# A recurrence planned among dense projections: key norms with tokens on partitions, two PSUM banks told apart, longer pauses, and one projection moved

## The chip, the cores and the metric

The kernel runs on one core of a Trainium2 chip. The metric is the device time of one execution in microseconds; the median of three runs of the kernel before is 1794.55 us (1793.61 to 1795.46). A change of less than 0.2% can't be told from none here.

## The reference, cut to what matters

One layer takes 1040 tokens (16 learned ones ahead of 1024) of width 1024 through a norm and one wide projection, two branches beside each other, an output projection, and a gated feed-forward part. The first branch is stick-breaking attention with 8 heads of 64; the second is a recurrence with 8 heads of 64. The lines on the recurrence that the change touches are these:

```python
rw = token_shift(rw, mu_rw[layer])
r, kr, vr, w_lo, a_lo, g_lo = jnp.split(rw, rw_splits, axis=-1)
w_log = -jax.nn.softplus(-(w0[layer] + jnp.tanh(w_lo) @ w_up[layer])) - 0.5
decay = jnp.exp(-jnp.exp(w_log.astype(jnp.float32)))
a = jax.nn.sigmoid(a0[layer] + a_lo @ a_up[layer])
g = jax.nn.sigmoid(g_lo) @ g_up[layer]
kk = split_heads((kr * k_k[layer]).astype(jnp.float32), RW_HEADS)
kk = kk / jnp.maximum(jnp.linalg.norm(kk, axis=-1, keepdims=True), 1e-12)
...
y_rw = rwkv7_recurrence(r_h, split_heads(decay, RW_HEADS), k_h, v_h, kk, a_h)
y_rw = group_norm_heads(y_rw, ln_x_w[layer], ln_x_b[layer])
```

The norm of a key is one number for each token and head.

## The kernel before

The start normalises the tokens and transposes them into `xhi` and `xlo`, a high and a low part; every dense projection is three matmuls (hi by hi, lo by hi, hi by lo) for each of eight slices of the width, in pieces of 346 or 348 tokens, or 512 where the 16 first tokens aren't needed. `wload` fetches a weight tile, casts its high part on ScalarE and subtracts for the low part (`wlo`) on VectorE, or on GpSimd once `LOP[0]` is set.

First come, each drained before the next, the column of the decay and of `a` (`wa`, lines 283 to 285), the gate (`g_cols`: two projections, their sigmoids, the splits of the results, then the products `psg`), and key, receptance and value of the first pair of heads. `LOP[0]` is set between `wa` and `g_cols`.

The recurrence runs in chunks of 64 tokens, for four pairs of heads, each in two units of 9 and 8 chunks: eight units. Three chains of steps work on them: `chain1` (`stage1`: decay, key norms, the matrices within each chunk), `chain2` (`stage2a`: the inverse of each chunk's triangular matrix, in which a small 16 by 16 inversion `Tt` is done on VectorE in 30 short instructions) and `chain3` (`stage2b`: the pass over the chunks, one `psC` step each, then a group norm and the transposes `psyT`). Every step ends in a `yield` of two numbers: its cost on TensorE and a pause. A planner (lines 719 to 745) keeps a clock of its own: it takes the next step of a chain whose pause is over, in the order chain3, chain2, chain1, and else one slice of a dense projection (`psm`, three matmuls, 3 x (columns + 34) / 2400). In this way the remaining 28 columns of the attention and its gates, and the next pairs' keys, receptances and values, fill the pauses. The order so found is fixed for TensorE alone; the other engines' orders are left to a scheduler. When the chains end, what is left of the dense work is drained, and the attention begins (`psv`, `psz`, then on VectorE the scan L795 and the product L796, the transposes `psaT`, the products `pso`).

PSUM is dealt out by tags: `mm` has 3 banks (dense), A has 2, B, C and S one each. Chain1 uses A, chain2 uses A and B in turn, chain3 and the attention use C and S.

The norm of the keys in `stage1` works on the keys' own layout, channels on partitions: the squares `sq` (128 by 576 or 512) are multiplied by `blk1`, whose two blocks of ones add up 64 channels and repeat each sum on 64 partitions; the square root, the maximum with 1e-12 and the reciprocal then run on the full 128 by 576 or 512, and the product `kkn` follows behind a pause of 20:

Of the kernel before, what the change touches and what calls it, by code (L numbers as in the profile page):

```python
# [13 lines left out]
AF = mybir.ActivationFunctionType  # L14
ALU = mybir.AluOpType
# [79 lines left out]
def _build(nc, tc, I, out, dbg, es):  # L95
# [183 lines left out]
    def drain(g):  # L279
        for _ in g:  # L280
            pass

    wa = rp.tile([128, LP], F32, name="wa")
    drain(proj_shift(I["win"][0], 0, wa))
    A.activation(wa[0:64], wa[0:64], AF.Tanh)

# [13 lines left out]
    def tl(nm, shape, tag=None, **kw):  # L300
        return rp.tile(shape, F32, tag=tag or nm, name=nm, **kw)
# [6 lines left out]
    def stage1(p, u, rkv):  # L308
# [12 lines left out]
        for a, m in pcs:  # L321
            ps = bank("A", "psw")
            T.matmul(ps[:, :m * 64], waup[0:64, 128 * p:128 * p + 128], wa[0:64, t0 + a * 64:t0 + (a + m) * 64],
                     start=True, stop=True)
            A.activation(sg[:, a:a + m, 1:65], u3(ps[:, :m * 64]), AF.Sigmoid, bias=CV(W0, p))
            ps = bank("A", "psa")
            T.matmul(ps[:, :m * 64], waup[64:128, 128 * p:128 * p + 128],
                     wa[64:128, t0 + a * 64:t0 + (a + m) * 64], start=True, stop=True)
            A.activation(at[:, a * 64:(a + m) * 64], ps[:, :m * 64], AF.Sigmoid, bias=CV(A0, p))
            yield 0.75, 1.2  # L330
        cc = tl("cc", [128, n, 65])
# [9 lines left out]

        nv = tl("nv", [128, w], "sg")
        kkn = tl("kkn", [128, w])
        for a, m in pcs:
            ps = bank("A", "psn")
            T.matmul(ps[:, :m * 64], blk1, sq[:, a * 64:(a + m) * 64], start=True, stop=True)
            A.activation(nv[:, a * 64:(a + m) * 64], ps[:, :m * 64], AF.Sqrt)
        for a in range(0, w, w // 4):
            sl = slice(a, a + w // 4)
            V.tensor_scalar(nv[:, sl], nv[:, sl], 1e-12, None, op0=ALU.max)  # L350
            V.reciprocal(nv[:, sl], nv[:, sl])
        yield 0.6, 20.0
        V.scalar_tensor_tensor(kkn, krs, CV(KK, p), nv, op0=ALU.mult, op1=ALU.mult)
        m1 = sq
# [19 lines left out]
        for c in range(0, n, 4):  # L374
            m = min(4, n - c)
            pss = [bank("A", "pss") for h in range(2)]
            for c_ in range(c, c + m):
                o = (c_ - c) * 128
                for h in range(2):
                    q = HQ[h]  # L380
                    T.matmul(pss[h][:, o:o + 128], BK[q, c_].rearrange("p s x -> p (s x)"), AV[q, c_, h:3:2 - h],
                             start=True, stop=True)
            late = 2.4 if m > 1 else 1.2
            for h in range(2):
# [22 lines left out]
    def stage2a(p, u, s1):  # L407
# [9 lines left out]
        for a in range(0, n, 8):  # L417
            m = min(8, n - a)
            ps = bank("B", "psW")
            for c in range(a, a + m):  # L420
                o = (c - a) * 64
                for h in range(2):
                    T.matmul(ps[HQ[h], o:o + 64], UA[HQ[1 - h], c, h], X[HQ[1 - h], c, h], start=True, stop=True)
            A.copy(X[:, a:a + m, 2], u3(ps[:, :m * 64]))
            yield 0.09 * m + 0.2, 1.2

# [21 lines left out]

        yield 0.0, 19.0
        R32 = [(h, b, slice(64 * h + 32 * b, 64 * h + 32 * b + 32)) for b in range(2) for h in range(2)]  # L450
        Xq = t2("Xq", [128, 9, 32], "Tt")
        ps = bank("B", "psU")
        for c in range(n):
            for h, b, rows in R32:
                T.matmul(ps[rows, c * 32:c * 32 + 32], UA[rows, c, h, 32 * b:32 * b + 32], TN[rows, c],
                         start=True, stop=True)
        yield 1.9, 1.3
        V.tensor_tensor(Xq[:, :n], ps[:, :n * 32].rearrange("p (c x) -> p c x", x=32),
                        qmask.unsqueeze(1).to_broadcast([128, n, 32]), op=ALU.mult)
        ps = bank("A", "psU2")  # L460
        for c in range(n):
            for h, b, rows in R32:
                T.matmul(ps[rows, c * 32:c * 32 + 32], Xq[rows, c], TT[rows, c, 32 * b:32 * b + 32],
                         start=True, stop=True)
        yield 1.9, 2.4
        pv = ps[:, :n * 32].rearrange("p (c x) -> p c x", x=32)
# [14 lines left out]
        for h in range(2):  # L481
            (A.copy, V.tensor_copy)[h](Xs[QB[h], :n], ps[QB[h], :n * 32].rearrange("p (c x) -> p c x", x=32))
        yield 1.0, 1.3
        ps = bank("A", "psX2")
        for c in range(n):
            for h in range(2):
                T.matmul(ps[QA[h], c * 32:c * 32 + 32], Xs[QB[h], c], TT[QB[h], c, 32:64], start=True, stop=True)
        for h in range(2):
            (A.copy, V.tensor_copy)[h](TT[QA[h], :n, 32:64], ps[QA[h], :n * 32].rearrange("p (c x) -> p c x", x=32))
        yield 1.0, 1.3  # L490

        Pt = t2("Pt", [128, 9, 64])
        GM = t2("GM", [128, 9, 128], "UA", bufs=3)
        for c in range(0, n, 4):
# [9 lines left out]
            for h in range(2):  # L504
                A.copy(X[HQ[h], c:c + m, h], pv[HQ[h], :, 1])
            yield 0.2 * m, 1.6
            ps = bank("A", "psEF")
            for c_ in range(c, c + m):
                o = (c_ - c) * 128
                for h in range(2):  # L510
# [5 lines left out]
                            op=ALU.add)  # L516
            yield 0.15 * m, 0.0
        return GM

    def stage2b(p, u, s1, GM, St):  # L520
# [5 lines left out]
        for c in range(n):  # L526
# [11 lines left out]
            if g > 0:  # L538
                o = (g - 1) % 8
                A.copy(Yt[64 * (o % 2):64 * (o % 2) + 64, o // 2], cp_[0:64, 0:128])  # L540
            yield 0.45, 1.3

# [48 lines left out]
    def g_cols():  # L591
# [20 lines left out]
        split(u3_[0:32], u3_[64:96], ur)  # L612
        A.copy(u3_[32:64], ur)
        for p in range(4):
            if p % 2 == 0:
# [53 lines left out]
    def chain3():  # L669
        St = None  # L670
        for i_ in range(NU):
            yield (lambda: i_ in st2), 1.6
            if i_ % 2 == 0:
                St = None
            St = yield from stage2b(i_ // 2, i_ % 2, st1[i_], st2[i_], St)
            yd[i_] = True
# [389 lines left out]
    with ExitStack() as s4:  # L1066
        w5 = pool(s4, "w5")
        ft = lambda nm, bufs, dt=F32: w5.tile([128, 512], dt, tag=nm, name=nm, bufs=bufs)
# [99 lines left out]
```

## Time and profile before

| | us |
|---|---|
| median of three runs | 1794.55 |
| the profiled execution | 1788.92 |
| its span | 1787.2 |
| TensorE busy | 1706.4 (95%) |
| VectorE busy | 1171.1 (66%) |
| ScalarE busy | 770.3 (43%) |
| GpSimd busy | 387.0 (22%) |

The profile is of one execution; times in it run from the span's start. The first 33 us hold the first norm and its transposes; the chains run from about 115 to 718 us; dense work alone follows to about 770; the attention and the branch projections to 1020, the output projection and the second norm to 1130, the feed-forward part to the end. In the rows below, PE is TensorE, DVE VectorE, ACT ScalarE, POOL GpSimd; PEld is the loading of weights into TensorE. What stands behind an arrow is what an engine waited for.

### The profile page before, as it was taken

How to read it: one execution, taken by the hardware profiler on the slowest of the kernel's cores; microseconds unless marked ns; L12 is line 12 of the kernel's file. 1: busy time of each engine (PE TensorE's matmuls, PEld its weight loads, DVE VectorE, ACT ScalarE, POOL GpSimd, SP SyncE). 2: the span in 40 equal slices, each digit the busy share in tenths (PEclk: the TensorE clock that was granted, in tenths of full speed). 3: DMA queues.
4: the chain of work that ended last, by engine and by line, in shares of the span. 5: the costliest groups of instructions: out<-in, count | busy, mean ns of one | idle time of the engine just before them, and what ended most of it. 6: DMA issues, size and time to landing. Idle time of an engine off the chain costs nothing.

```text
span 1787.2 us, 28844 instructions
## 1 busy us (share of the span) xinstructions
PE 1706.4 (95%) x11120; PEld 1407.7 (79%) x11120; DVE 1171.1 (66%) x1969; ACT 770.3 (43%) x1542; POOL 387.0 (22%) x393
## 2 busy tenths in 40 slices
PE   7999999999999999998989999999999999999998
PEld 6787888888897788866666887788888888778886
DVE  6345654655655632078988844898887877579756
ACT  7344354444545533256655323532333332254445
POOL 2222112211111221300000001365454544210000
PEclk9999989999999999999999999999999999999999
DMA  5223213211211354225422535133333323297233
GB/s 173 71 77 97 70 49 95 57 54 40 80 41 50 94 127 127 89 74 129 119 72 63 180 129 189 50 116 100 107 118 100 106 89 100 93 323 250 89 107 129
DMA packets 98249, 188.79 MB, mean 106 GB/s; under 512 B 38592, under 2 KB 40912, under 8 KB 98112
## 3 DMA queue, kind: packets, MB, share of 16 engines
q1 hardware_dynamic: 83536, 139.63, 26.5%
q0 software_dynamic: 14576, 47.32, 7.0%
q8 instruction: 88, 1.44, 0.3%
q14 instruction: 49, 0.40, 0.1%
HBM read 133.49 MB, written 53.41 MB: 105 GB/s over the span
## 4 chain that ended last, share of the span: by engine, by line
PE 76%; DVE 12%; ACT 5%; issue 4%; DMA 3%; SPq 1%; POOL 0%; ACTq 0%; DVEq 0%; POOLq 0%
PE psf L959 8%; PE psf L958 8%; PE psm L254 8%; PE psf L957 8%; PE psm L255 7%; PE psm L256 7%; PE psfo L1120 4%; PE psfo L1121 4%; PE psfo L1119 4%; DVE ub L795 3%; DVE be L796 2%; PE psC L530 1%; PE pso L814 1%; PE psaT L804 1%; PE pswo L906 1%
## 5 line engine op out<-in xcount | busy, mean ns | idle before, releaser
L254 PE MATMUL psm<-xhi,whi 128*128 128x346 f32 (+3 forms) x872 | 326.8, 375 | 2.6 <-DVE stagel L147 1.8
L255 PE MATMUL psm<-xlo,whi 128*128 128x346 f32 (+3 forms) x872 | 308.7, 354 | 0.3 <-DVE xlo L147 0.3
L256 PE MATMUL psm<-xhi,wlo 128*128 128x346 f32 (+3 forms) x872 | 308.5, 354 | 0.0
L254 PEld LDWEIGHTS psm<-xhi,whi 128*128 128x128 f32 (+1 forms) x872 | 166.0, 190 | 30.4 <-issue 10.7
L256 PEld LDWEIGHTS psm<-xhi,wlo 128*128 128x128 f32 (+1 forms) x872 | 165.5, 190 | 15.5
L255 PEld LDWEIGHTS psm<-xlo,whi 128*128 128x128 f32 (+1 forms) x872 | 166.2, 191 | 13.8 <-DVE xlo L147 0.7
L156 POOL TENSOR_TENSOR wlo<-wraw,whi 128x1024 fp32r<-128x1024 f32 (+1 forms) x42 | 100.3, 2389 | 290.7 <-ACT whi L155 257.4
L1119 PE MATMUL psfo<-wh,ah 128*128 128x512 f32 x308 | 120.7, 392 | 2.5 <-ACT wh L146 2.5
L1120 PE MATMUL psfo<-wl,ah 128*128 128x512 f32 x308 | 121.0, 393 | 2.2 <-DVE wl L147 2.2
L1121 PE MATMUL psfo<-wh,al 128*128 128x512 f32 x308 | 120.8, 392 | 0.0
L146 ACT CAST sh<-S 128x512 fp32r<-128x512 f32 x88 | 54.5, 622 | 144.5 <-PE psf L958 135.8
L155 ACT CAST whi<-wraw 128x1024 fp32r<-128x1024 f32 (+2 forms) x71 | 67.0, 943 | 96.6 <-PE psm L255 36.0
L795 DVE TENSOR_TENSOR_SCAN ub<-ub 128x144 f32<-128x144 f32 (+7 forms) x64 | 87.7, 1381 | 4.2 <-ACT ub L792 4.2
L1047 DVE TENSOR_TENSOR g<-g,sg 128x512 f32<-128x512 f32 x44 | 78.4, 1781 | 15.5 <-ACT sg L1046 14.0
L146 ACT CAST ah<-ar 128x512 fp32r<-128x512 f32 x77 | 47.9, 622 | 92.5 <-PE psfo L1120 58.7
L147 DVE TENSOR_TENSOR al<-ar,ah 128x512 fp32r<-128x512 f32 x77 | 56.5, 734 | 42.4 <-ACT ah L146 42.3
L156 DVE TENSOR_TENSOR wlo<-wraw,whi 128x512 fp32r<-128x512 f32 (+1 forms) x29 | 28.4, 979 | 74.8 <-ACT whi L155 74.8
L147 DVE TENSOR_TENSOR sl<-S,sh 128x512 fp32r<-128x512 f32 x85 | 74.8, 881 | 0.0
L1119 PEld LDWEIGHTS psfo<-wh,ah 128*128 128x128 f32 x308 | 58.4, 190 | 15.1 <-ACT wh L146 2.9
L1120 PEld LDWEIGHTS psfo<-wl,ah 128*128 128x128 f32 x308 | 58.4, 190 | 14.6 <-DVE wl L147 2.5
L1121 PEld LDWEIGHTS psfo<-wh,al 128*128 128x128 f32 x308 | 58.4, 190 | 12.2
L536 DVE TENSOR_SCALAR Sbd<-psC,gam 64x64 f32<-64x64 f32 x64 | 18.5, 289 | 74.5 <-PE psC L533 73.8
(386 smaller groups left out, 4197.0 us busy)
## 6 DMA issues: line engine op xcount, KB each, us to landing
wr<-in_wffi SPq DMA_DIRECT2D x46, 512.0 KB, 3.6
wraw<-in_win SPq DMA_DIRECT2D x42, 512.0 KB, 3.9
ar<-d_a SPq DMA_DIRECT2D x77, 256.0 KB, 2.8
d_a<-sa POOLq DMA_DIRECT2D x44, 256.0 KB, 2.8
wf<-in_wffo SPq DMA_DIRECT2D x44, 256.0 KB, 5.3
d_a<-sg POOLq DMA_DIRECT2D x33, 256.0 KB, 2.4
d_g<-stage POOLq DMA_DIRECT2D x32, 256.0 KB, 3.1
gt<-d_g SPq DMA_DIRECT2D x32, 256.0 KB, 2.6
```

Source lines behind the costliest of these rows:

```text
L147: V.tensor_tensor(lo, src, hi.bitcast(F32), op=ALU.subtract)
L156: (G if LOP[0] else V).tensor_tensor(lo, raw, hi.bitcast(F32), op=ALU.subtract)
L254: T.matmul(ps[:M, :n], hv[:, k], xhi[:, k, t0:t0 + n], start=(k == 0), stop=False)
L255: T.matmul(ps[:M, :n], hv[:, k], xlo[:, k, t0:t0 + n], start=False, stop=False)
L256: T.matmul(ps[:M, :n], lv[:, k], xhi[:, k, t0:t0 + n], start=False, stop=(k == 7))
L795: V.tensor_tensor_scan(rv, rv, rv, 1.0, op0=ALU.mult, op1=ALU.bypass)
L957: T.matmul(ps, wa_[0][:, kc], xa_[0][:, k], start=(k == 0), stop=False)
L958: T.matmul(ps, wa_[0][:, kc], xa_[1][:, k], start=False, stop=False)
L959: T.matmul(ps, wa_[1][:, kc], xa_[0][:, k], start=False, stop=(k == 3))
L1119: T.matmul(ps, ah[:, tt], wh, start=(i == 0), stop=False)
L1120: T.matmul(ps, ah[:, tt], wl, start=False, stop=False)
L1121: T.matmul(ps, al[:, tt], wh, start=False, stop=(i == NP - 1))
```

## The change

It has five parts. The projection of `wa` and its Tanh move into `g_cols`, between the splits and the products `psg`. The key norms get tokens on partitions: a block of 96 (or 128) tokens of `sq` is the stationary operand and two columns of `blk1` the moving one, so one small matmul gives the block's norms for two heads; root, maximum and reciprocal run on 96 by 12 (or 128 by 8); ScalarE copies them out to 64 columns each (`bt`); and a new step of transposes (`psnt`, six or four a unit) brings them to the keys' layout, where `kkn` reads them from PSUM. `psU2`, `psX2` and `psEF` of chain2 move from bank tag A to B. The planner's pauses change, most of them upwards. The pool `w5` of the last stage is laid at the other side of the memory.

```diff
     wa = rp.tile([128, LP], F32, name="wa")
-    drain(proj_shift(I["win"][0], 0, wa))
-    A.activation(wa[0:64], wa[0:64], AF.Tanh)
...
-            yield 0.75, 1.2
+            yield 0.75, 2.0
...
-        nv = tl("nv", [128, w], "sg")
+        tb = 96 if n == 9 else 128
+        nb = w // tb
+        nv = tl("nv", [128, 6, 2])[:tb, :nb]
+        bt = tl("bt", [128, 9, 2, 64], "BK").rearrange("p c s x -> p (c s x)")[:tb, 0:nb * 128]
         kkn = tl("kkn", [128, w])
-        for a, m in pcs:
-            ps = bank("A", "psn")
-            T.matmul(ps[:, :m * 64], blk1, sq[:, a * 64:(a + m) * 64], start=True, stop=True)
-            A.activation(nv[:, a * 64:(a + m) * 64], ps[:, :m * 64], AF.Sqrt)
-        for a in range(0, w, w // 4):
-            sl = slice(a, a + w // 4)
-            V.tensor_scalar(nv[:, sl], nv[:, sl], 1e-12, None, op0=ALU.max)
-            V.reciprocal(nv[:, sl], nv[:, sl])
-        yield 0.6, 20.0
-        V.scalar_tensor_tensor(kkn, krs, CV(KK, p), nv, op0=ALU.mult, op1=ALU.mult)
+        ps = bank("A", "psn")
+        pv = ps[:tb, 0:2 * nb].rearrange("p (b h) -> p b h", h=2)
+        for b in range(nb):
+            T.matmul(pv[:, b], sq[:, b * tb:(b + 1) * tb], blk1[:, 0:128:64], start=True, stop=True)
+        A.activation(nv, pv, AF.Sqrt)
+        V.tensor_scalar(nv, nv, 1e-12, None, op0=ALU.max)
+        V.reciprocal(nv, nv)
+        A.copy(bt.rearrange("p (b h x) -> p b h x", h=2, x=64), nv.unsqueeze(3).to_broadcast([tb, nb, 2, 64]))
+        yield 0.2 * nb, 3.4
+        for a in range(0, nb, nb // 2):
+            ps = bank("A", "psnt")
+            for b in range(a, a + nb // 2):
+                T.transpose(ps[:, (b - a) * tb:(b - a + 1) * tb], bt[:, 128 * b:128 * b + 128], ident[:tb, :tb])
+            sl = slice(a * tb, (a + nb // 2) * tb)
+            V.scalar_tensor_tensor(kkn[:, sl], krs[:, sl], CV(KK, p), ps[:, :nb // 2 * tb], op0=ALU.mult, op1=ALU.mult)
+        yield 0.11 * nb, 14.0
...
-            late = 2.4 if m > 1 else 1.2
+            late = 3.0 if m > 1 else 2.0
...
-        yield 1.9, 1.3
+        yield 1.2, 2.0
...
-        ps = bank("A", "psU2")
+        ps = bank("B", "psU2")
...
-        yield 1.9, 2.4
+        yield 1.2, 3.0
...
-        yield 1.0, 1.3
-        ps = bank("A", "psX2")
+        yield 0.9, 2.0
+        ps = bank("B", "psX2")
...
-            yield 0.2 * m, 1.6
-            ps = bank("A", "psEF")
+            yield 0.25 * m, 2.2
+            ps = bank("B", "psEF")
...
-            yield 0.15 * m, 0.0
+            yield 0.25 * m, 1.9
...
-            yield 0.45, 1.3
+            yield 0.45, 1.4
...
+
+        drain(proj_shift(I["win"][0], 0, wa))
+        A.activation(wa[0:64], wa[0:64], AF.Tanh)
         for p in range(4):
...
-            yield (lambda: i_ in st2), 1.6
+            yield (lambda: i_ in st2), 0.5
...
-        w5 = pool(s4, "w5")
+        w5 = pool(s4, "w5", side="right")
```

Line numbers differ between the two kernels behind line 283. The first place is TensorE at the gate's products, before; `psm` with 32 rows is the second gate projection, L621 to L623 are the parts of `psg` that need the first one's split, and L624 is the part that needs the second one's:

```order
L256 MATMUL psm<-xhi,wlo 32x346
L621 MATMUL psg<-gpr,gat 128x512
...
L623 MATMUL psg<-gpr,gcc 128x512
L624 MATMUL psg<-gUA,gsq 128x512 x5
L621 MATMUL psg<-gpr,gat 128x512
```

After the change the same place reads so (L632 to L635 are the old L621 to L624):

```order
L255 MATMUL psm<-xlo,whi 32x346
L256 MATMUL psm<-xhi,wlo 32x346
L254 MATMUL psm<-xhi,whi 128x348
...
L256 MATMUL psm<-xhi,wlo 128x346
L632 MATMUL psg<-gpr,gat 128x512
L633 MATMUL psg<-gAV,gat 128x512
L634 MATMUL psg<-gpr,gcc 128x512
L635 MATMUL psg<-gUA,gsq 128x512
```

The 72 matmuls of `wa`, with 128 rows, now stand between the second gate projection and its first use; before, they stood ahead of both.

The second place is ScalarE at the norm of the first unit, before; `E` and `cc` are the two exponentials of the decay, `nv` the roots of the norms, `gam` the decay at the ends of chunks:

```order
L334 ACT_TABLE_LOAD
L334 ACTIVATE E<-cc 128x585
L347 ACT_TABLE_LOAD
L347 ACTIVATE nv<-psn 128x320
L336 ACT_TABLE_LOAD
L336 ACTIVATE cc<-cc 128x9x64
L340 COPY gam<-E 64x9 x2
L347 ACT_TABLE_LOAD
L347 ACTIVATE nv<-psn 128x256
L146 CAST stageh<-psm 128x512
```

After the change (the copy `bt` reads the reciprocals that VectorE makes of `nv`, and the transposes `psnt` read `bt`):

```order
L332 ACT_TABLE_LOAD
L332 ACTIVATE E<-cc 128x585
L350 ACT_TABLE_LOAD
L350 ACTIVATE nv<-psn 96x12
L334 ACT_TABLE_LOAD
L334 ACTIVATE cc<-cc 128x9x64
L338 COPY gam<-E 64x9 x2
L353 COPY bt<-nv 96x768
L146 CAST stageh<-psm 128x512
```

Four table loads became three, and the exponential `cc` and the copies `gam` stand between the small root and the copy that TensorE's new step needs.

The third place is TensorE at the end of the chains, before; `psC` is a step over one chunk, `psyT` the transposes behind the last group norm, `psv` the attention's first instruction:

```order
L530 MATMUL psC<-X,UB 128x64 x2
L533 MATMUL psC<-Sbd_352,GM 128x128
L254 MATMUL psm<-xhi,whi 128x512
...
L256 MATMUL psm<-xhi,wlo 128x512
L558 MATMUL psyT<-ident,Yt 128x128 x4
L254 MATMUL psm<-xhi,whi 128x512
...
L256 MATMUL psm<-xhi,wlo 128x512
L762 MATMUL psv<-ident,vt 16x128
```

After the change (`psz`, `psaT` and `pso` are of the attention):

```order
L256 MATMUL psm<-xhi,wlo 128x512
L538 MATMUL psC<-X,UB 128x64 x2
L541 MATMUL psC<-Sbd_351,GM 128x128
L538 MATMUL psC<-X,UB 128x64 x2
L773 MATMUL psv<-ident,vt 16x128
...
L541 MATMUL psC<-Sbd_352,GM 128x128
L815 MATMUL psaT<-ident,be 16x128
...
L815 MATMUL psaT<-ident,be 128x128 x3
L566 MATMUL psyT<-ident,Yt 128x128 x4
L799 MATMUL psz<-kh,qs 128x264
L800 MATMUL psz<-kl,qs 128x264
L825 MATMUL pso<-aT_7657,vn 64x128
```

Before, 222 dense matmuls follow the last `psyT`. After, the last dense matmul stands ahead of the first of the last unit's eight `psC` steps; the other seven and `psyT` are placed among the attention's first instructions, and the first `pso` behind `psyT`.

## Rows read from the trace of the kernel before

**Rows 1.** Stretches: length; busy PE, PEld, DVE, ACT, POOL (instructions); clock; DMA.

```profile
160.00:660.00 500.00, 475.33 (x4618) 411.72 (x4618) 290.73 (x737) 237.93 (x484) 91.31 (x95) 0.97 0.24 66
720.00:765.00 45.00, 45.00 (x196) 36.38 (x195) 1.19 (x2) 8.41 (x13) 11.41 (x11) 1.00 0.28 91
765.00:1020.00 255.00, 232.71 (x1745) 175.96 (x1744) 217.96 (x317) 146.33 (x407) 1.93 (x7) 1.00 0.38 108
770.00:810.00 40.00, 36.14 (x288) 26.17 (x287) 39.48 (x60) 30.75 (x92) 0.89 (x4) 1.00 0.31 92
```

**Rows 2.** Waits of TensorE: releaser, us in total, times, longest.

```profile
PE psg L624 <- DVE gUA L147: 3.6, 1, 3.6
...
PE psa L327 <- ACT TT L469: 2.5, 2, 1.3
PE psn L346 <- DVE TT L489: 2.4, 2, 2.0
```

**Rows 3.** Narrow stretches: length, busy TensorE (instructions), granted clock, DMA share, GB/s.

```profile
66.30:73.10 6.80, 5.93 (x14) 0.50 0.36 146
250.60:260.80 10.20, 9.80 (x88) 0.50 0.13 46
547.60:551.00 3.40, 3.40 (x21) 0.51 0.00 0
```

**Rows 4.** Timeline of TensorE at the gate's products: start, duration, row.

```profile
63.14 0.40 PE L623 MATMUL psg<-gpr,gcc 128*128 128x512 f32 x1
67.17 2.47 PE L624 MATMUL psg<-gUA,gsq 96*128 96x512 f32 x5 [3.63 <-DVE gUA L147]
```

**Rows 5.** Groups by line: weight splits on two engines, reciprocal of the norms.

```profile
L156 POOL TENSOR_TENSOR wlo<-wraw,whi 128x1024 fp32r<-128x1024 f32 (+1 forms) x42 | 100.3, 2389 | 290.7 <-ACT whi L155 257.4 <-PE psC L533 17.8 <-PE psU L455 12.2
L351 DVE RECIPROCAL nv<-nv 128x144 f32<-128x144 f32 (+1 forms) x32 | 29.7, 968 | 0.0
L156 DVE TENSOR_TENSOR wlo<-wraw,whi 128x512 fp32r<-128x512 f32 (+1 forms) x29 | 28.4, 979 | 74.8 <-ACT whi L155 74.8
```

**Rows 6.** Timeline of ScalarE at the second unit's norm.

```profile
167.00 0.64 ACT L334 ACTIVATE E<-cc 128x520 f32<-128x520 f32 x1
...
168.01 0.63 ACT L336 ACTIVATE cc<-cc 128x512 f32<-128x512 f32 x1
...
169.09 1.28 ACT L347 ACT_TABLE_LOAD   x1
170.38 0.66 ACT L347 ACTIVATE nv<-psn 128x256 f32<-128x256 f32 x2
```

**Rows 7.** Timeline of VectorE at the same place.

```profile
166.58 0.14 DVE L435 TENSOR_TENSOR Tm<-Z,Tt 72x15 f32<-72x15 f32 x1
...
168.98 0.68 DVE L368 TENSOR_TENSOR AV<-r,E 128x512 f32<-128x512 f32 x1
```

**Rows 8.** Timeline of TensorE: second unit's last psa and psn; four transposes.

```profile
164.44 0.38 PE L327 MATMUL psa<-wa,waup 64*128 64x256 f32 x1
...
166.62 1.02 PE L346 MATMUL psn<-sq,blk 128*128 128x256 f32 x4
...
192.60 0.60 PE L394 MATMUL pst<-ident,AV 128*128 128x128 f32 x4
```

**Rows 9.** Timeline of all engines: last unit's steps, its norm's two ends.

```profile
703.72 0.55 PE L530 MATMUL psC<-X,UB 128*128 128x64 f32 x4
...
704.11 0.44 PE L533 MATMUL psC<-Sbd,GM 128*128 128x128 f32 x2
...
704.59 0.29 DVE L536 TENSOR_SCALAR Sbd<-psC,gam 64x64 f32<-64x64 f32 x1 [1.76 <-PE psC L533]
...
704.91 0.31 ACT L537 ACTIVATE Sbd<-psC,gam 64x64 f32<-64x64 f32 x1 [1.46 <-DVE Sbd L536]
...
708.72 0.26 ACT L540 COPY Yt<-psC 64x128 f32<-64x128 f32 x1 [0.66 <-PE psC L533]
...
717.63 0.60 PE L558 MATMUL psyT<-ident,Yt 128*128 128x128 f32 x4
```

More of the change, by code (lines that the diff above doesn't have):

```diff
@@ L424, in stage2a @@
             A.copy(X[:, a:a + m, 2], u3(ps[:, :m * 64]))
-            yield 0.09 * m + 0.2, 1.2
+            yield 0.09 * m + 0.2, 1.8
         Z = t2("Z", [128, 288], "Z")[:npb, 0:256].rearrange("p (i t) -> p i t", t=16)
@@ L447, in stage2a @@
             SY.dma_start(TT[rows, :n, 16 * b:16 * b + 16], dt_[ib].rearrange("c j t -> j c t"))
-        yield 0.0, 19.0
+        yield 0.0, 20.0
         R32 = [(h, b, slice(64 * h + 32 * b, 64 * h + 32 * b + 32)) for b in range(2) for h in range(2)]
@@ L489, in stage2a @@
             (A.copy, V.tensor_copy)[h](TT[QA[h], :n, 32:64], ps[QA[h], :n * 32].rearrange("p (c x) -> p c x", x=32))
-        yield 1.0, 1.3
+        yield 0.9, 2.0
         Pt = t2("Pt", [128, 9, 64])
```

## The prediction

> **What bounds the kernel now.** I read the stretches of the span first [rows 1]. While the chains run, 160 to 660 us, TensorE is busy 475.33 of 500: it is the bound, with 24.7 us of holes. From 720 to 765 it does dense work alone, 45.00 of 45, while VectorE has 1.19 of work; 196 matmuls of 512 columns in 45 us are 0.23 us each. In the attention TensorE is busy 232.71 of 255 and VectorE 217.96, and in its first 40 us VectorE 39.48 of 40: there VectorE is the bound. So a change to the recurrence is worth what it takes out of TensorE's holes and work, less what it pushes into the attention.
>
> The list of TensorE's waits [rows 2] then says what the holes are: one of 3.6 us at the gate's products, and in the chains many of about 1 us, two of them for chain1's `psa` and `psn` waiting for the copies into `TT` that chain2 makes out of bank A: 2.5 and 2.4 us. The narrow stretches [rows 3] show that a hole costs more than itself: from 66.3, from 250.6 and from 547.6 us the granted clock is 0.50 (1.2 instead of 2.4 GHz), for 6.8, 10.2 and 3.4 us, each just behind a hole or with one in it. Between 138 and 660 us there are eight such dips: seven like the last row and one of 10.2, 34.1 us in all, of which half, 17, is lost. Holes and dips of the chains come to 42 us.
>
> **The change part by part.**
>
> *The projection of `wa`.* The gate's products stood until 67.17, 3.63 us, for the split of the second gate projection [rows 4], and the clock then was half for 6.8 us, worth 3.4: 7.0 together. In the new order 72 matmuls of 346 or 348 columns, about 11 us (72 x 0.23 x 346/512), come between that projection and the products. They move within a stretch where TensorE is full, so they cost nothing, and 11 us cover 3.63. The dip goes with the hole: -7.0. If a hole stays in part, the dip may too: -3 to -7. Against it stands that the first weights now have their low part made by GpSimd, at 2389 ns in the mean against 979 on VectorE [rows 5]; at most those 1.4 us show if the first projection waits for it. It has the start's other transposes beside it, so I take +0.5 (0 to 1.4).
>
> *Key norms, TensorE.* Four records of `psn` take 1.02 us [rows 8]; the 32 of eight units, 8.2 us, go. In come 6 or 4 matmuls a unit, 40 in all, of two columns and in float32, which the trace shows as two passes. The nearest row is `psC`: its four passes of 64 columns start 0.39 us before the next row [rows 9], so 0.098 each: 40 x 2 x 0.098 = 7.8. The 40 transposes cost 0.44 us for four (the row's 0.60 overlaps the next by its fill) [rows 8]: 4.4. One more step in each unit breaks the dense stream once more, an estimated 0.25 x 8 = 2. Sum +6.0. Ends: with two columns at no cost at all -2, with a pass at twice the 64-column one +14; I take +6, since the row is near.
>
> *Key norms, VectorE.* 32 reciprocals of 968 ns, 29.7 us [rows 5], go, and the maxima before them. VectorE isn't the bound here, 290.73 of 500 [rows 1], so the time itself is worth nothing: it pays only where TensorE waited for a result behind them, which is in the holes. The dense work hides it either way; without that cover it would be worth at most those 29.7.
>
> *Key norms, the new wait.* TensorE's new step `psnt` waits for `bt`. On ScalarE, `E` took 0.64 from 167.00, `cc` 0.63, the copies of `gam` 0.45 to the next row, a table load 1.28 [rows 6]. `E` began 2.2 us behind the last `psa` (164.44 + 0.38) [rows 8]. After `E` the new order has load, small root, load, `cc`, `gam`, `bt`: 1.28 + 0.33 (half of the two roots' 0.66) + 1.28 + 0.63 + 0.45 + 0.65 (a copy of one 128x512 form, about as `cc`) = 4.6. So `bt` ends about 7.4 us behind `psa`. In the new order, between the same points stand 24 dense matmuls and `psn` for the first unit, 24 x 0.23 + 1.2 = 6.7; the others have 6.3 to 7.8. In units with a small inversion beside it, the maximum and reciprocal stand behind `Tt` on VectorE: eleven of its thirty instructions take from 166.58 to 168.98 [rows 7], 0.22 each, 6.5 in all, which makes it 9 to 10. I get holes of 0 to 2.3 us, some 8 us over eight units, and three or four dips behind them of 1.7 each: 6. What is queued behind `psnt` on TensorE is dense work that nothing hinders, so a hole here is a whole loss.
>
> The Trainium skill ("ScalarE: Activation LUTs", section "What ACT_TABLE_LOAD costs") states 1283 ns for the load and about 1380 ns of drain more for each change of table set. The row agrees with the first and not with the second: load at 169.09, root at 170.38 [rows 6]. By the page the two loads in the new path would cost 2.8 us more a unit; its case is among the rivals.
>
> *Banks and pauses.* With `psU2`, `psX2` and `psEF` in bank B, chain1 no longer waits for chain2's copies: the 2.5 and 2.4 of [rows 2] and the dips behind them go. Chain2's steps now wait for each other's evacuation, one copy, at most the 0.64 of the 128x520 form in [rows 6], that the longer pauses (2.0 to 3.0 for 1.2 to 2.4) cover. The other holes are of the size of those in [rows 2], a result that comes some 1 us late behind a pause of 1.2 to 1.6; 0.7 us more should close most of them. I leave 5 us of these and one dip of 2. With the 14 of `psnt` that is 21 of the 42: -21. Ends: nothing but the banks gained, -8; only a fourth left, -33.
>
> *The end of the chains.* The longer pauses use up dense work earlier. Before, 222 dense matmuls, 222 x 0.23 = 51 us, ran behind the last `psyT`; now all of the last unit's chunks and its group norm stand behind the last dense one. A chunk's chain goes from `psC` at 704.11 through VectorE at 704.59 to the end of ScalarE at 704.91 + 0.31: 1.11, with the next matmul 1.2 us. Eight make 9.6. The norm takes from 708.72 to 717.63, 8.9 [rows 9]. This was under dense work and is now open for 18.5 us, save for the attention's own first work beside it, `psz`, scans and `psaT`, which need nothing from it. What can't be hidden is VectorE's share, since VectorE is full there [rows 1]: 8 x 0.29 for `Sbd` and six passes of 0.68 [rows 7, 9], 6.4 us. Then `pso` waits for `psyT` on bank C and `psaT` for bank S, so VectorE is not filled throughout: I add 4 for that and 2 for the steps that wait in TensorE's queue behind scans. +12. Ends: half of VectorE's work hidden in its small gaps, 4; the whole chain open, with each step behind a scan of attention, 9.6 + 8.9 and 8 x 1.2 more, 28.
>
> *The pool `w5`* changes addresses only; the casts for the last stage wait for the same sigmoid: 0 (-1 to +1).
>
> Sum: -7.0 + 0.5 + 6.0 - 21 + 12 = -9.5. It is made against the profiled execution, 1788.92 (span 1787.2 and 1.7 around it), which is 5.6 below the median 1794.55; from the median the forecast is 1785.
>
> **The rivals.**
>
> B. The pauses cover everything, `psnt` too, and the tail hides: -7 + 0.5 + 6 - 33 + 5 = -28.5, 1766. For it: the holes are small [rows 2]. Against it: 7.4 against 6.7 at `psnt`.
>
> C. The last unit's chain decides and the kernel gets slower: with seven `psC` steps strung through TensorE's queue, each waits for VectorE behind a scan, and everything of the attention behind it in the queue waits too. At 28 instead of 12 the sum is +6.5, 1801. It decides from a tail of about 22. For it: VectorE 39.48 of 40. Against: scans of the first blocks are short.
>
> D. Each of the two changes of table ahead of `bt` holds ScalarE for as long again as the load's 1.28 [rows 6]: 2 x 1.28 x 8 = 20.5 us more of holes, so +11, 1806. Against it: the root starts at 170.38, right behind the load from 169.09 [rows 6]. That is the case which the Trainium skill's page on ScalarE, named above, would make.
>
> E. The holes only move: each longer pause lets another step come late, chain2's single bank makes new waits, and holes and dips stay near 34. Then -7 + 0.5 + 6 - 8 + 12 = +3.5; with a cheaper tail 0: 1794 to 1798. The change would do what it says and gain nothing.
>
> **How the numbers follow.** My forecast (own range 1779 to 1792) has 0.45, B 0.20, E 0.15, C 0.15, D 0.05. A measurement tells 0.2%, 3.6 us, from no change. Faster: 0.41 + 0.20 + 0.02 = 0.63. Same: 0.04 of the forecast, 0.11 of E and 0.03 of C, 0.18. Slower: 0.02 of E, 0.12 of C and D's 0.05, 0.19. The range of 8 in 10 reaches from B's 1766 to C's 1801.
>
> **What would show it.** The gate: no wait of over 0.5 us at the products, and clock 1.00 from 66 to 73. Norms: `psn` in two-column records near 0.1 us a pass, `psnt` waits for `bt` some 8 us in the list of waits. Chains: holes near 13 us where 24.7 were, three to five dips for eight. Tail: the stretch from the last dense matmul to the first `pso` is some 20 us, and the attention's end stands about 12 us later against its first `psv`. Wrong would be a `psnt` that never waits (B), one of 3 us and more each unit (D), new waits of `psPQ` or `psX` for bank B (E), or a first `pso` over 25 us behind the last dense matmul (C).

## The result, and the profile after

The changed kernel takes 1780.32 us (median of 4 runs, 1779.6 to 1782.14) against 1794.08 for the kernel before in the same comparison: 13.8 us less, ratio 0.993 with a 95% interval of 0.9918 to 0.9942. The forecast was 1785, 9.5 us less. The two profiled executions, 1788.92 and 1779.6, differ by 9.3. The 4.5 between the two differences is spread: single executions of the kernel before lay between 1784 and 1798 us in the comparisons of this study, and the profiled one is at the fast end.

Three marks split the profiled difference, spans 1787.2 and 1777.8. The first `psw` of the chains starts at 111.8 before and 106.6 after: -5.2. From there to the attention's first `psv` it takes 657.8 and 639.7: -18.1. From that to the last `pso` it takes 208.6 and 222.9: +14.3. The rest is the same within 0.4.

The gate first. TensorE's timeline after, where the products follow the projection of `wa`:

```profile
61.09 0.32 PE L256 MATMUL psm<-xhi,wlo 128*128 128x346 f32 x1
61.25 0.39 PE L632 MATMUL psg<-gpr,gat 128*128 128x512 f32 x1
...
61.94 0.40 PE L635 MATMUL psg<-gUA,gsq 96*128 96x512 f32 x1
```

There is no hole; in [rows 4] it was 3.63 us. L635, the part that needs the second split, follows three matmuls later. The products start at 61.25 instead of 59.88: 1.4 us went to the start, more than the 0.5 I had taken; 0.63 of it is a wait of `psm` at 17.6 for the low part that GpSimd makes, and the rest isn't explained by a row.

The stretches after (columns as in [rows 1]), the second of them the chains' end:

```profile
160.00:660.00 500.00, 479.17 (x4565) 415.96 (x4566) 251.25 (x633) 230.30 (x460) 101.04 (x102) 0.99 0.24 68
...
745.00:770.00 25.00, 18.96 (x123) 15.24 (x121) 20.51 (x41) 18.76 (x53) 1.04 (x4) 0.86 0.22 70
```

While the chains run, TensorE's holes are 20.8 us of 500, where they were 24.7 [rows 1]: hardly less. VectorE has 251 us of work there for 291. The last unit's steps and the attention's start now share the 25 us from 745, where TensorE is busy 19.0 and VectorE 20.5.

The narrow stretches with half clock (columns as in [rows 3]); the first is the old dip at the gate, the next three are all there are in the chains, the last is in the chains' open end:

```profile
66.30:73.10 6.80, 6.80 (x39) 6.34 (x39) 2.96 (x5) 0.41 (x1) 1.80 (x5) 1.00 0.92 369
480.10:483.50 3.40, 2.77 (x9) 2.38 (x10) 2.00 (x4) 0.95 (x3) 0.00 (x0) 0.50 0.22 20
579.10:582.50 3.40, 3.40 (x19) 2.53 (x19) 2.96 (x5) 1.68 (x2) 0.00 (x0) 0.50 0.08 22
644.00:647.40 3.40, 3.40 (x10) 2.63 (x9) 3.35 (x6) 1.61 (x3) 0.54 (x1) 0.50 0.26 83
760.00:766.80 6.80, 4.80 (x24) 3.80 (x24) 5.57 (x10) 6.08 (x13) 0.00 (x0) 0.50 0.11 39
```

Eight dips of 34.1 us in the chains became three of 10.2, at a loss of about 5 us for 17, and the one at the gate is gone. So in these two executions it was the clock that gave most of the 18.1 us back, not the holes: 12 of it, and 4 from the holes. (The last unit's `psC` steps, some 5 us of TensorE's work, moved behind the mark, and the norms' new matmuls took 3.6.)

The waits of TensorE after (releaser, total, times, longest):

```profile
PE psnt L358 <- ACT bt L353: 11.4, 6, 4.4
...
PE psX L495 <- DVE Xs L490: 3.5, 1, 3.5
...
PE psPQ L509 <- DVE Tm L443: 1.8, 2, 0.9
```

`psa` and `psn` no longer wait for `TT`, as they did in [rows 2]; the largest wait is now the new step's, 11.4 us in six waits. The 3.5 us of `psX`, for the copy `Xs`, end at 577.4, ahead of the second of the three dips.

The norm of the first unit on ScalarE after, to set beside [rows 6]:

```profile
112.54 0.69 ACT L332 ACTIVATE E<-cc 128x585 f32<-128x585 f32 x1
113.25 1.28 ACT L350 ACT_TABLE_LOAD   x1
114.54 0.18 ACT L350 ACTIVATE nv<-psn 96x12 f32<-96x12 f32 x1
114.74 1.28 ACT L334 ACT_TABLE_LOAD   x1
116.03 0.69 ACT L334 ACTIVATE cc<-cc 128x576 f32<-128x576 f32 x1
...
117.17 0.83 ACT L353 COPY bt<-nv 96x768 f32<-96x768 f32 x1
```

and on TensorE:

```profile
112.49 1.10 PE L349 MATMUL psn<-blk,sq 128*96 128x2 f32 x12
...
118.06 0.71 PE L358 MATMUL psnt<-ident,bt 96*128 96x96 f32 x6 [0.88 <-ACT bt L353]
```

Load, root, load, `cc`, the copies of `gam`, `bt`: from 113.25 to 118.0, 4.75 us, where the prediction had 4.6. `psnt` started 0.88 late. The twelve records of `psn` cost 1.10 us, 0.09 each: 7.3 for 80; with the transposes, 6 in 0.71, some 4.5 for 40, and 8.2 taken away, the norms cost TensorE 3.6 us more, not 6.

The two longest waits of `psnt`, 4.42 and 3.24, come from something else, and not from the same. ScalarE ahead of the first of them:

```profile
473.01 0.64 ACT L332 ACTIVATE E<-cc 128x520 f32<-128x520 f32 x1 [1.68 <-DVE cc L330]
...
473.77 1.28 ACT L593 ACT_TABLE_LOAD   x1
475.06 0.60 ACT L593 ACTIVATE stage<-psm 128x512 f32<-128x512 f32 x1
475.68 1.28 ACT L334 ACT_TABLE_LOAD   x1
...
479.34 0.18 ACT L350 ACTIVATE nv<-psn 128x8 f32<-128x8 f32 x1
...
480.07 0.61 ACT L353 COPY bt<-nv 128x512 f32<-128x512 f32 x1
```

Between the two exponentials `E` and `cc` stands a sigmoid of a dense gate column (`stage`), with a table load of its own at 473.77; the exponential then needs another at 475.68. These 3.2 us delay the root to 479.34 and `bt` to 480.7. Ahead of the second wait no sigmoid stands between `E` and `bt`: there `E` itself is late, because VectorE starts the running sum `cc`, which `E` reads, only at 636.08.

```profile
636.08 1.24 DVE L330 TENSOR_TENSOR_SCAN cc<-rmask,sg 128x520 f32<-128x520 bf16 x1
```

```profile
637.35 0.64 ACT L332 ACTIVATE E<-cc 128x520 f32<-128x520 f32 x1 [2.92 <-DVE cc L330]
```

VectorE was at the small inversion `Tt` until 634.4 and then at a copy and two passes over the `Yt` of a group norm. The half-clock stretches from 480.1 and 644.0 begin at the end of the first and just behind the second of these waits.

The end of the chains after, to set beside [rows 9]; the first row is the last dense matmul:

```profile
745.01 0.39 PE L256 MATMUL psm<-xhi,wlo 128*128 128x512 f32 x1
745.24 0.55 PE L538 MATMUL psC<-X,UB 128*128 128x64 f32 x4
...
763.96 1.06 PE L566 MATMUL psyT<-ident,Yt 128*128 128x128 f32 x4
...
765.89 1.10 PE L825 MATMUL pso<-aT,vn 128*64 128x128 f32 x8 [0.43 <-ACT Yt L568]
```

The first `pso` stands 20.9 us behind the last dense matmul.

### The profile page after: what moved, and what is told of

It reads as the page before. It is cut to its first block, busy times and chain, and to the rows that moved or that the text cites. A ratio compares the mean times of both kernels' runs of the same rounds, so it can differ in the third digit from the quotient of the medians.

```text
span 1777.8 us, 28970 instructions
## 1 busy us (share of the span) xinstructions
PE 1700.5 (96%) x11208; PEld 1402.0 (79%) x11208; DVE 1148.9 (65%) x1928; ACT 767.8 (43%) x1539; POOL 388.8 (22%) x394
## 4 chain that ended last, share of the span: by engine, by line
PE 73%; DVE 13%; issue 5%; ACT 5%; DMA 2%; POOL 1%; SPq 0%; DVEq 0%; POOLq 0%; ACTq 0%
PE psf L970 8%; PE psf L969 8%; PE psf L968 8%; PE psm L254 8%; PE psm L256 7%; PE psm L255 7%; PE psfo L1131 4%; PE psfo L1132 4%; PE psfo L1130 4%; DVE ub L806 4%; DVE be L807 2%; PE pswo L916 2%; PE pswo L917 2%; PE pswo L918 2%; PE pso L825 1%
## 5 line engine op out<-in xcount | busy, mean ns | idle before, releaser
L254 PE MATMUL psm<-xhi,whi 128*128 128x346 f32 (+4 forms) x872 | 325.2, 373 | 0.5 <-ACT xhi L146 0.5
L256 PE MATMUL psm<-xhi,wlo 128*128 128x346 f32 (+4 forms) x872 | 306.2, 351 | 0.6 <-POOL wlo L156 0.6
L255 PE MATMUL psm<-xlo,whi 128*128 128x346 f32 (+4 forms) x872 | 305.9, 351 | 0.1
L254 PEld LDWEIGHTS psm<-xhi,whi 128*128 128x128 f32 (+1 forms) x872 | 163.6, 188 | 29.7 <-issue 13.7
L155 ACT CAST whi<-wraw 128x1024 fp32r<-128x1024 f32 (+1 forms) x71 | 66.8, 943 | 114.7 <-issue 54.2
L815 PE MATMUL psaT<-ident,be 128*128 128x128 f32 (+1 forms) x352 | 57.1, 281 | 13.7 <-DVE be L807 9.5
```

The source lines that it names most:

```text
L254: T.matmul(ps[:M, :n], hv[:, k], xhi[:, k, t0:t0 + n], start=(k == 0), stop=False)
L255: T.matmul(ps[:M, :n], hv[:, k], xlo[:, k, t0:t0 + n], start=False, stop=False)
L256: T.matmul(ps[:M, :n], lv[:, k], xhi[:, k, t0:t0 + n], start=False, stop=(k == 7))
```

## The experiments

Each was compared with the kernel before on the same chip in at least four timed executions; "the changed kernel" is the 1780.3 above. The median of before was 1792.2 to 1793.5 in them.

**The projection of `wa` alone.**

```diff
 (kernel before)
-    drain(proj_shift(I["win"][0], 0, wa))
-    A.activation(wa[0:64], wa[0:64], AF.Tanh)
...
         A.copy(u3_[32:64], ur)
+        drain(proj_shift(I["win"][0], 0, wa))
+        A.activation(wa[0:64], wa[0:64], AF.Tanh)
```

> The kernel before with the projection of wa moved alone. Theory (the gate's hole and the half clock behind it go, the first weights' split on GpSimd costs a little): -6.5 + 1.3 = -5.2 against before, about 1789. Rival (the later stages swallow it, since the chains start earlier by 5 us but wait for the same things): 1794, no change.

Measured 1786.74 for 1792.6, ratio 0.9969 (0.9957 to 0.9981): -5.9. The theory holds, and it is the -5.2 of the profile.

**The old norms in the changed kernel.**

```diff
 (changed kernel)
-            T.matmul(pv[:, b], sq[:, b * tb:(b + 1) * tb], blk1[:, 0:128:64], start=True, stop=True)
...
-        yield 0.11 * nb, 14.0
+        for a, m in pcs:
+            ps = bank("A", "psn")
+            T.matmul(ps[:, :m * 64], blk1, sq[:, a * 64:(a + m) * 64], start=True, stop=True)
+            A.activation(nv[:, a * 64:(a + m) * 64], ps[:, :m * 64], AF.Sqrt)
...
+        yield 0.6, 18.0
```

> The changed kernel with the old key norms (channels on partitions, one pause of 18 behind them); all else as changed. Theory N (the new norms cost TensorE 4 us of work, 11.4 us of waits at psnt and two half-clock dips worth 3.4, and relieve only VectorE, which is not the bound): 8 to 14 us faster than the changed kernel, 1766 to 1772. Rival V (VectorE's 37 us fewer are what lets the pauses hold; with the reciprocals back, results come late and the holes return): 1780 to 1790.

Measured 1790.95, ratio to before 0.9989 (0.9979 to 0.9999): 10.6 us slower than the changed kernel. Theory N falls; the time lies 1 us above the range of rival V. The waits of TensorE:

```profile
PE psX L486 <- DVE Xs L481: 12.4, 2, 6.5
...
PE psPQ L500 <- DVE TT L488: 4.5, 1, 4.5
```

and VectorE ahead of the first of them (start, duration, row, and what ended its idle time):

```profile
421.99 0.38 DVE L349 TENSOR_SCALAR nv<-nv 128x144 f32<-128x144 f32 x2 [0.92 <-ACT nv L346]
422.29 1.96 DVE L350 RECIPROCAL nv<-nv 128x144 f32<-128x144 f32 x2
426.11 0.38 DVE L349 TENSOR_SCALAR nv<-nv 128x144 f32<-128x144 f32 x2 [1.87 <-ACT nv L346]
426.41 1.96 DVE L350 RECIPROCAL nv<-nv 128x144 f32<-128x144 f32 x2
428.40 0.43 DVE L481 COPY Xs<-psX 32x256 f32<-32x256 f32 x1
```

The copy `Xs`, for which `psX` waits 6.48 us, stands in VectorE's queue behind two pairs of maxima and reciprocals, and the second pair waits 1.87 us for ScalarE's second root. Either the 5 us of work or the wait for the root could be what costs; the next two runs tell them apart.

**The work of the reciprocals put back, with nothing waiting for a root.**

```diff
 (changed kernel)
         V.reciprocal(nv, nv)
...
+        ex = tl("ex", [128, 144])[:tb]
+        for q_ in range(4):
+            V.tensor_scalar(ex, sq[:tb, 0:144], nv[:, 0, 0:1], None, op0=ALU.max)
+            V.reciprocal(ex, ex)
         yield 0.2 * nb, 3.4
```

> The changed kernel with four maxima and four reciprocals of 144 columns more in each unit on VectorE, right behind the small ones, on a scratch tile that nothing reads: 32 x 0.97 + 32 x 0.27 = 39.6 us of VectorE work, the order of TensorE and its pauses as changed. Theory V (VectorE's short but late work is what the old norms cost): 6 to 12 us slower than the changed kernel, 1786 to 1792, with new waits at psX, psPQ or pss. Rival S (the old norms are slower because of the single pause of 18 and the roots on ScalarE, not of VectorE): 1780 to 1783.

Measured 1783.44, ratio to before 0.9942 (0.9925 to 0.9959). TensorE's waits, and two stretches:

```profile
PE psnt L362 <- ACT bt L353: 11.6, 6, 4.5
...
PE psX L499 <- DVE Xs L494: 3.5, 1, 3.5
```

```profile
160.00:660.00 500.00, 478.90 (x4488) 415.58 (x4487) 287.97 (x690) 230.23 (x460) 100.16 (x102) 0.99 0.24 68
761.00:781.50 20.50, 17.41 (x81) 12.79 (x82) 16.20 (x24) 13.99 (x37) 0.00 (x0) 0.50 0.16 52
```

VectorE has its 37 us back, 288 for 251, and TensorE waits as in the changed kernel: 11.6 for 11.4, 3.5 for 3.5. The 3 us on the median have nothing to do with it as far as the profile shows: this execution had a half-clock stretch of 20.5 us behind the chains' end, the changed kernel's one of 6.8, with the same holes. At one and the same mean granted clock, 0.987, an execution took 1780.8 us here, and two took 1780.8 and 1782.1 in the changed kernel. Theory V falls.

**The old norms without the root.**

```diff
 (kernel with the old norms)
-            A.activation(nv[:, a * 64:(a + m) * 64], ps[:, :m * 64], AF.Sqrt)
+            A.copy(nv[:, a * 64:(a + m) * 64], ps[:, :m * 64])
```

> The run with the old key norms in the changed kernel (1791), with the square root left out: a plain copy stands for it, so the keys are divided by the square of their norm. The reciprocals stay on VectorE, two table loads a unit go from ScalarE. Theory R (the old norms cost what they do because VectorE's queue stands at the maximum until ScalarE's second root, which comes behind two table changes, and chain2's copy Xs stands behind it in that queue): psX waits for Xs fall from 12.4 to under 4 us, the dips behind them go, 1778 to 1784. Rival V2 (the reciprocals' own 36 us in front of chain2's copies are it): psX waits stay over 8, 1787 to 1792.

Measured 1774.2, ratio to before 0.9896 (0.9877 to 0.9915): 16.8 us faster than with the root.

```profile
PE psX L486 <- DVE Xs L481: 6.3, 2, 3.4
```

The waits of `psX` went from 12.4 to 6.3, not under 4, and the time fell below what theory R gave. So half of these waits is left with the reciprocals alone, and the roots with their table changes made the other half and most of the time. The old norms' price in the changed kernel is the roots on ScalarE with their table changes; rival V2 falls by the time, though not wholly by the waits. How much of that price comes through VectorE's queue behind the roots, and how much through ScalarE's other results, this run doesn't part.

**The norms alone**, in the kernel before (edit: the norm's lines of the diff above and its two yields).

> The kernel before with the new key norms alone (pauses 3.4 and 14 in place of 20; banks, other pauses and wa as before). Theory V (reciprocals on VectorE held up chain2's small copies and the splits of dense results; without them the holes behind go): 5 to 10 us faster than before, 1783 to 1788. Rival N (new transposes wait, more work on TensorE, VectorE not the bound): 1793 to 1800.

Measured 1789.21, ratio 0.9981 (0.9966 to 0.9995): -3.0, between the two. With the old pauses `psnt` waits 9.2 us in seven waits, and `psC` 7.4, where it waited 0.5 before: part of the gain is spent there.

**The banks alone.**

```diff
 (kernel before)
-        ps = bank("A", "psU2")
+        ps = bank("B", "psU2")
...
-        ps = bank("A", "psX2")
+        ps = bank("B", "psX2")
...
-            ps = bank("A", "psEF")
+            ps = bank("B", "psEF")
```

> The kernel before with psU2, psX2 and psEF in bank B alone; pauses as before. Theory (chain1 waited for chain2's copies out of bank A): psa <- TT 2.5 and psn <- TT 2.4 go with the two dips behind them, worth up to 6.8: 1784 to 1789. Rival (with short pauses the single bank B makes new waits as long as the old): 1792 to 1798.

Measured 1803.13, ratio 1.0052 (1.0037 to 1.0067): 10.5 slower, worse than the rival.

```profile
PE psPQ L501 <- DVE GM L515: 7.8, 6, 2.4
PE psPQ L501 <- DVE TT L489: 6.9, 1, 6.9
PE psPQ L501 <- DVE Tt L437: 5.1, 3, 2.9
PE psPQ L501 <- DVE Tm L435: 4.9, 3, 2.3
```

The waits of `psa` and `psn` for `TT` are gone, as the theory said, but `psPQ` waits 24.7 us in all; before, it waited 2.9. One of these, 6.9, is for its input `TT`. The others fit a piece of `psPQ` that stands behind the evacuation of `psEF` into `GM`, in the same bank, and that evacuation behind what VectorE is doing, the inversion (`Tm`, `Tt`) above all.

**The old pauses in the changed kernel** (edit: each yield of the diff but the norms' two set back).

> The changed kernel with the pauses and costs of before in every yield but the two of the key norms. The parts measured so far add up like this: against before, wa -5.9, old norms put back +10.7, banks alone +9.4, all together -13.8; so the pauses would be worth -13.8 + 5.9 + 10.7 - 9.4 = -6.6 if the parts add. Theory A (they add): 7 us slower than the changed kernel, about 1787, with psPQ waiting for bank B's evacuation as in the banks-alone run. Rival (the longer pauses are what makes the bank move and the norms work at all): 1793 or more. Other rival (the shorter pauses leave 117 dense matmuls behind the last psyT, which hides the tail's 12 and outweighs the holes): 1780 or less.

Measured 1792.74, ratio to before 1.0003 (0.9989 to 1.0017): 12.4 slower than the changed kernel. The parts do not add; the first rival, that the longer pauses are what makes the bank move and the norms work, comes nearest. Its attention took 210.0 us from the first `psv` to the last `pso`, as before, since 117 dense matmuls remained behind the last `psyT`: the open end is worth some 13 us and the chains' waits more, with `psPQ` at 13.2 us for 1.8, `psnt` at 9.3 and `psC` at 5.7.

**The pool `w5` on its old side** (edit: `side="right"` taken out).

> The changed kernel with the pool w5 on its old side. Theory: its addresses alone change, no wait: 1780, within 1.5 us of the changed kernel. Rival (the last stage's first weights could be fetched or cast earlier on one side): 2 to 5 us off, with the waits of psfo for wh and wl other than 2.5 and 2.2.

Measured 1782.44, ratio to before 0.9947 (0.9929 to 0.9964), an interval that overlaps the changed kernel's. `psfo` waits 2.5 and 2.0, near the 2.5 and 2.2 of the changed kernel. Between no effect and some 3 us the medians don't decide; at a mean granted clock of 0.987 an execution took 1780.8 us here too, which speaks for none.

**A longer pause ahead of `psnt`.**

```diff
 (changed kernel)
-        yield 0.2 * nb, 3.4
+        yield 0.2 * nb, 6.4
...
-        yield 0.11 * nb, 14.0
+        yield 0.11 * nb, 11.0
```

> The changed kernel with the pause ahead of psnt 6.4 for 3.4 and the one behind it 11 for 14. Theory (psnt's wait is a pause too short by some 1 to 4 us): its 11.4 us fall under 3, the dips behind it go, the last unit's chain lies some 3 us further in the open: 1768 to 1773. Rival (what is late is late for another reason, or the shorter pause behind it makes pss wait instead): 1778 to 1784.

Measured 1774.05, ratio 0.9892 (0.9879 to 0.9906): -6.3 against the changed kernel.

```profile
PE psnt L358 <- ACT bt L353: 3.7, 3, 1.8
```

The wait fell from 11.4 to 3.7, and TensorE's holes between 160 and 660 us from 20.8 to 11.2. The theory holds in its direction; the wait stayed above 3, and the time lies 1 us above its range and below the rival's.

**The norms ahead of the decay.** `psn`, root, reciprocal and `bt` move into the first step with `psw` and `psa`, and `psnt` into the one behind the second.

```diff
 (changed kernel)
             A.activation(at[:, a * 64:(a + m) * 64], ps[:, :m * 64], AF.Sigmoid, bias=CV(A0, p))
+            if a == 0:
...
+                ps = bank("A", "psn")
...
+                A.copy(bt.rearrange("p (b h x) -> p b h x", h=2, x=64), nv.unsqueeze(3).to_broadcast([tb, nb, 2, 64]))
             yield 0.75, 2.0
...
-        yield 0.2 * nb, 3.4
```

> The changed kernel with psn in the first psw and psa step (behind its psa) and psnt in the step behind the second one, with the pause of 14; the step with the pause of 3.4 is gone. Theory (the root, reciprocal and copy then have a whole step of dense work more; the chain of each unit is some 4 us shorter, so that 12 to 87 dense matmuls remain among the last unit's steps): psnt waits under 2 us of 11.4, the two dips behind them gone, the tail 5 to 8 us cheaper: 1760 to 1768. Rival (a table load more in each unit, or pss late behind a pause too short): 1775 to 1785.

Measured 1775.33, ratio 0.9916 (0.9891 to 0.994): faster, but at the edge of the rival's range.

```profile
PE psn L337 <- ACT sg L323: 7.0, 7, 2.0
...
PE psa L325 <- DVE bon L411: 2.5, 1, 2.5
```

`psnt` waits 0.3 us; `psn` waits instead, for a bank of tag A that a sigmoid still reads.

**The same, with `psn` in the bank of `psa`.**

```diff
 (kernel with the early norms)
-                ps = bank("A", "psn")
-                pv = ps[:tb, 0:2 * nb].rearrange("p (b h) -> p b h", h=2)
+                pv = ps[:tb, 480:480 + 2 * nb].rearrange("p (b h) -> p b h", h=2)
...
-        yield 0.11 * nb, 14.0
+        yield 0.11 * nb, 12.5
```

> The kernel with the early norms, with psn put into spare columns of the bank that psa has just written, and the pause behind psnt 12.5 for 14. Theory (the run with early norms traded the waits at psnt, 11.4, for waits at psn and psa for a third bank of tag A: 6.4 in six waits of psn and 2.5 of psa; these go, and 24 dense matmuls in place of 12 stand behind the last psC): 6 to 10 us faster than the early norms, 1764 to 1770. Rival (waits move on to pss behind the shorter pause, or to psn for its squares): 1772 to 1780.

Measured 1777.57, ratio 0.9907 (0.989 to 0.9925): the theory falls.

```profile
PE psa L336 <- ACT at L327: 13.5, 8, 3.1
```

The columns are spare, but the tile isn't: the norm's matmuls (here under the name `psa`) wait until ScalarE has read the tile for `at`, in all eight units.

**The same, with `psn` in a bank of the dense work.**

```diff
 (kernel with the early norms)
-                ps = bank("A", "psn")
+                ps = bank("mm", "psn")
...
-        yield 0.11 * nb, 14.0
+        yield 0.11 * nb, 13.0
```

> The kernel with the early norms, with psn in a bank of tag mm (the dense one, of three) and the pause behind psnt 13 for 14. Theory (psn's six waits for a third bank of tag A, 6.4, and psa's of 2.5 for the bon behind it go, and mm has a bank to spare while a dense piece runs): 1765 to 1771, the fastest of all. Rival (dense matmuls then wait for a bank behind the root, or the extra table load in each unit makes other results late): 1773 to 1780.

Measured 1767.24 (1762.65 to 1771.85), ratio 0.9854 (0.983 to 0.9878): 25.8 us faster than before and 13.1 faster than the changed kernel, the best of the study.

```profile
PE psX L488 <- ACT TT L477: 5.4, 3, 2.4
...
PE psnt L358 <- ACT sg L323: 1.5, 2, 1.3
```

```profile
160.00:660.00 500.00, 484.54 (x4719) 420.19 (x4718) 267.90 (x674) 240.95 (x476) 100.58 (x102) 1.00 0.26 72
```

TensorE is busy 484.5 of 500 at a granted clock of 1.00, with no dip in the chains at all.

**Which part took the holes, and which the dips.** The same stretch, 160 to 660 us, with the norms alone, with the old norms in the changed kernel, and with the old pauses in it (columns as in [rows 1]):

```profile
160.00:660.00 500.00, 474.60 (x4611) 412.07 (x4611) 257.34 (x656) 228.32 (x463) 94.17 (x97) 0.99 0.24 67
```

```profile
160.00:660.00 500.00, 472.45 (x4397) 409.33 (x4395) 282.54 (x673) 234.38 (x465) 100.36 (x101) 0.98 0.24 67
```

```profile
160.00:660.00 500.00, 468.82 (x4599) 406.11 (x4599) 260.74 (x668) 223.14 (x455) 94.92 (x96) 0.99 0.24 68
```

| 160 to 660 us | holes of TensorE, us | at half clock, us |
|---|---|---|
| kernel before | 24.7 | 30.7 |
| norms alone | 25.4 | 13.7 |
| banks alone | 35.2 | 47.8 |
| changed kernel | 20.8 | 10.2 |
| old norms in the changed kernel | 27.6 | 20.5 |
| old pauses in the changed kernel | 31.2 | 6.8 |

The new norms took half of the dips away or more, alone as well as in the changed kernel. The longer pauses, with the new norms in place, took holes away, some 10 us, and no dips that show. Each row is one execution, and the half clock differs between executions of one order (41.0 us with `wa` alone, whose chains are those of before, and 13.7 twice in the order of the changed kernel). The mean granted clock, known for every execution, agrees: its median is 0.983 before, 0.988 with the norms alone and 0.991 with the old pauses.

## Why the prediction was right, point by point

The sum of -9.5 came within 0.2 us of the profiled difference, 9.3, and that is luck in part: terms were off by 1 to 5 us in both directions, and some 5 us of `psC` work that left the chains' stretch had no term. Against the medians, 13.8, it was 4 us short.

*The gate:* -7.0 + 0.5 was forecast; -5.2 in the profile, -5.9 alone. The mechanism is as told; the start's term was too small, 1.4 for 0.5. Its bound of 1.4 came from means over different shapes [rows 5]; in the shape that both engines have, 128x1024, the split takes 2.43 us on GpSimd and 1.35 on VectorE.

*TensorE's work for the norms:* +6.0 forecast, 3.6 from the rows after. The row of 64 columns was near: 0.09 a pass for 0.098. The 2 us for breaking the dense stream can't be seen apart.

*The wait at `psnt`:* 8 us and 6 for dips forecast, 11.4 and two dips worth 3.4 measured. The size was right in part by luck: the path of 4.6 us was 4.75, but 7.7 of the 11.4 us are two waits of which one came from a gate's sigmoid with its table load, and the other from a running sum that stood on VectorE behind the small inversion and the passes of a group norm. The prediction had the inversion in the way of the maximum and the reciprocal, not of `E`, and no sigmoid.

*VectorE's relief, taken at nothing:* right as far as the work goes, since 37 us put back changed no wait. But the step that counted a norm's cost only as work and the new wait failed in its comparison with the old: it said in effect that the old norms, with the new pauses, would be some 20 us better, and they are 10.6 worse. What it left out is the two full-width roots in two places of ScalarE's queue, each with its table change, for which VectorE's queue stood still. It didn't show in the sum, because the dips that the new norms took away (half clock 30.7 to 13.7 us, norms alone) stood there under banks and pauses.

*Banks and pauses:* -21 forecast for holes and dips together, 16 measured (24.7 + 17 before, 20.8 + 5 after). Of that only 4 are holes; the prediction had expected 13 us of holes left and 20.8 are. It was right that a hole can cost more than itself: before, 3.4 us at half clock, 1.7 of them lost, followed a hole of 0.97 at 139.1. It was wrong on where the dips went: half of them or more went with the new norms, and none that shows with the pauses. That the banks by themselves gain was wrong, with the sign: alone they cost 10.5.

*The open end:* +12 forecast, +14.3 measured, about 5 of it from two dips, 6.8 us from 760 and 3.4 from 855.6, that [rows 1] of the attention did not have. The first `pso` came 20.9 us behind the last dense matmul, some 20 forecast.

*`w5`:* 0 forecast; the medians don't tell it from up to 3, executions at the same clock speak for 0.

The rivals: B fell with 11.4 us of waits at `psnt` and an end that cost 14.3 where it had 5. C fell: the end cost 14, not 28. D fell at 114.54, where the root starts right behind the load from 113.25. The Trainium skill ("ScalarE: Activation LUTs", section "What ACT_TABLE_LOAD costs") states 1283 ns for the load and some 1380 of drain; the loads here are 1.28 us, and no drain follows any of those shown. E was right on the holes, which stayed near their size, and wrong on the time, since the dips did not stay.

What stays open: why holes of 1.2 to 1.7 us at 170.8, 191.1 and 272.2 in the changed kernel were followed by no dip while smaller ones were before. One execution of each kernel can't tell it.

## What to carry to other kernels

A value that one engine needs soon is priced by the queues that it passes, not by the work in it: here two roots a unit with their table changes cost 16.8 us, and 37 us of reciprocals off the bound engine nothing that shows. Parts of a change to a planned order aren't additive; the same bank move cost 10 us with short pauses and stands in a faster kernel with long ones. What it is worth there is not shown, since no run has the long pauses without it. When a small result can be made before the long chain that it doesn't depend on, do it there, and give it a bank of the stream that has one to spare.

## What the runs showed of the hardware

A half-clock stretch behind one and the same pattern of holes, at the chains' end, was 6.8 us long in the changed kernel's profiled execution and 20.5 in those of two kernels with the same order there: some 7 us that no instruction explains.
